# One core, one decoder block: u and y_a with its gate by token, q, k and y_b's gate in merged 512-column matmuls

## The chip, the core and the metric

The kernel runs on one core of one Trainium2 chip. Its time is the device time of one execution in microseconds (us). An execution under the profiler gives a trace: every instruction of the engines with its start and duration. The engines are TensorE (PE, matmuls and transposes), VectorE (DVE), ScalarE (ACT), GpSimd (POOL) and SyncE (SP, which here issues the DMAs of the weights). Each works through its own queue in order and waits on semaphores for the others.

## What is computed

One decoder block for 256 tokens with 1024 features, in float32. Cut to what the change touches:

```python
h = rms_norm(x, norm_mix_g[i])
proj = h @ w_in[i]                       # 1024 x 7168
za_u, za_v, q, k, v_att, g_a, g_b = jnp.split(proj, offsets, axis=-1)
y_a = sgu_mixer(gelu(za_u), gelu(za_v), ...)     # u * (tril(W_s) layer_norm(v) + b), per chunk of 128 tokens
y_b = moba_attention(heads(q), heads(k), heads(v_att), rel_bias)   # 16 heads of 64, causal
merged = sigmoid(g_a) * y_a + sigmoid(g_b) * y_b
x = x + merged @ w_out[i]
x = x + square(relu(rms_norm(x) @ w_ff1[i])) @ w_ff2[i]
gate = sigmoid(rms_norm(x) @ w_ple_gate[i])
x = x + gate * (p[i] @ w_ple_proj[i])
return rms_norm(x, norm_final_g)
```

## The kernel before

**Exact products from three.** Every large matmul is made of operands split into a rounded part and a rest (hi and lo for weights, index 0 and 1 for activations): hi x hi + hi x lo + lo x hi. Weights arrive in tiles of 128 x 2048 (1 MB), 69 of them in the order of the list `ORDER`, on SP's queue (`load_to`, L73). ACT rounds a tile in two pieces of 1024 columns (hi, L84), DVE subtracts (lo, L85). `weights(key, width, ahead=3)` (L95) asks for the tile of a step and has the tiles up to two steps ahead split; there are four buffers for raw tiles and three each for hi and lo.

**Two forms of a projection.** `proj_T` (L215) makes output by feature: the weights stand still, 256 token columns move, three matmuls for each of eight k blocks (`mm3`, L116 to L119), twice 128 features per tile. `proj_tok` (L227) makes output by token: 128 tokens stand still and 512 weight columns move (`tok3`, L121 to L128). The first MLP product (`ff1_mm`, L574) has a third form: by feature, with both parts of the activations moving as one matmul of 512 columns against hi, then 256 columns against lo; ACT copies the 512 sums to SBUF (`z`, L584) and DVE adds the two halves (L606).

**The stages around the change.** (1) v by token (`v_rows`). (2) 1/rms of x is spread over columns by a matmul with ones (L272) and copied to `R0`; u by feature in four `proj_T` calls from x times its gain, each multiplied by R0 on DVE and sent through gelu on ACT. At the same time ACT and DVE make a normalised, split copy of x (`hT`). (3) q in four calls from hT; between them v's layer norm and the spatial mixing (`mix`, L362), which multiplies into u. (4) Two halves J of eight heads each: k in two calls (`keys`), v by token in one `proj_tok` call, then four gate calls (20 is y_a's gate, 24 is y_b's gate). Attention goes in pairs of heads c, four pairs for each half, between the matmuls of the projections (the `mid` functions run on PE between the two feature blocks of a call): scores into the pool `scores` (two buffers of two PSUM banks each), softmax on DVE and ACT (`s`), `att_normalise` on DVE, `att_transpose` on PE with a copy by ACT to `pt`, `att_values` on PE. `merge(j)` adds both gated parts and splits them into `mT`. (5) The output projection, whose accumulators take the banks of the pool `scores` after that is closed (L510), then the MLP and the rest.

PSUM has eight banks: three for projections (`mm`), one `yb`, four for the scores. All queues follow the order in which the code is written.

Of the kernel before, what the change touches and what calls it, by code (L numbers as in the profile page):

```python
# [50 lines left out]
def block_kernel(ctx: ExitStack, tc: tile.TileContext, xt, xk, pt, rows, wst, bsp, rel, buckets, wts, out):  # L51
# [63 lines left out]

    def mm3(o, wh, wl, x, first, last, **kw):  # L116
        nc.tensor.matmul(o, wh, x[:, 0], start=first, stop=False, **kw)  # L117
        nc.tensor.matmul(o, wh, x[:, 1], start=False, stop=False, **kw)  # L118
        nc.tensor.matmul(o, wl, x[:, 0], start=False, stop=last, **kw)  # L119
# [107 lines left out]
    def proj_tok(name, c, x, mid=None):  # L227

        os_ = [bank(shape=(P, 512)) for t in range(2)]
        for i in range(2):  # L230
# [1 line left out]
            for k in range(4):
                tok3(os_, x[:, 4 * i + k], wh[:, k], wl[:, k], i + k == 0, i == 1 and k == 3)
            if i == 0 and mid:
                mid()
        return os_
# [33 lines left out]
    rb = bank("yb", 1)  # L270
    for t in range(2):
        nc.tensor.matmul(rb[:, 0, t * P:(t + 1) * P], ones, dg[:, t], start=True, stop=True)  # L272
    R0 = small.tile([P, S], F32, tag="R", name="R0", bufs=1)
    nc.scalar.activation(R0, rb[:, 0], AF.Copy)


    sgu_a = act.tile([P, 2, D], F32, tag="kT", name="sgu_a")
# [599 lines left out]
```

## Time and profile before

| | |
|---|---|
| median of 3 runs | 429.25 us (429.21 to 429.41) |
| the profiled execution | 429.07 us |
| its span (first to last instruction) | 427.4 us |
| granted TensorE clock, mean | 0.996 |
| TensorE busy | 417.5 us (98%), 2556 matmuls in the records |
| VectorE busy | 278.4 us (65%) |
| ScalarE busy | 233.5 us (55%) |
| DMA | 82.02 MB, mean 192 GB/s |

A busy share of PE says little by itself, because matmuls overlap: the next one starts before the one ahead has ended. The distance between starts is what one costs in a stream. The stages lie in the span as follows: v from 5.9 us, u from 29, q from 53, the two halves of attention from 83 to 188, the output projection to 212, the MLP to 390.

### The profile page before, as it was taken

How to read it: one execution, taken by the hardware profiler on the slowest of the kernel's cores; microseconds unless marked ns; L12 is line 12 of the kernel's file. 1: busy time of each engine (PE TensorE's matmuls, PEld its weight loads, DVE VectorE, ACT ScalarE, POOL GpSimd, SP SyncE). 2: the span in 40 equal slices, each digit the busy share in tenths (PEclk: the TensorE clock that was granted, in tenths of full speed). 3: DMA queues.
4: the chain of work that ended last, by engine and by line, in shares of the span. 5: the costliest groups of instructions: out<-in, count | busy, mean ns of one | idle time of the engine just before them, and what ended most of it. 6: DMA issues, size and time to landing. Idle time of an engine off the chain costs nothing.

```text
span 427.4 us, 6272 instructions
## 1 busy us (share of the span) xinstructions
PE 417.5 (98%) x2556; PEld 370.4 (87%) x2556; DVE 278.4 (65%) x373; ACT 233.5 (55%) x365; POOL 9.4 (2%) x18
## 2 busy tenths in 40 slices
PE   8999999999999999999999999999999999999992
PEld 7789999998999989998888888888888888888882
DVE  3676889675585755945578866666666666646555
ACT  5685544276464555564346666555555555435824
POOL 1001020000000000000000000000000000000001
PEclk9999999999999999999999999999999999999998
DMA  7999539545433444465353676555545455552002
GB/s 268 425 393 393 200 128 383 214 166 198 149 138 120 186 140 163 165 275 185 111 166 115 217 285 224 199 199 196 194 179 186 181 186 184 184 196 87 1 2 98
DMA packets 13692, 82.02 MB, mean 192 GB/s; under 512 B 1541, under 2 KB 1813, under 8 KB 5088
## 3 DMA queue, kind: packets, MB, share of 16 engines
q1 hardware_dynamic: 12384, 78.12, 49.9%
q0 software_dynamic: 848, 2.96, 1.9%
q10 hardware_dynamic: 432, 0.54, 0.4%
q8 instruction: 20, 0.33, 0.3%
q14 instruction: 8, 0.07, 0.0%
HBM read 80.54 MB, written 1.07 MB: 191 GB/s over the span
## 4 chain that ended last, share of the span: by engine, by line
PE 90%; DMA 4%; ACT 2%; issue 1%; DVE 1%; POOL 0%; SPq 0%; POOLq 0%; ACTq 0%
PE mm_t L578 13%; PE mm_t L117 9%; PE mm_t L118 9%; PE mm_t L119 9%; PE mm_t L580 7%; PE y L125 7%; PE y L128 7%; PE y L127 7%; DMA raw<-wts 4%; PE o L125 2%; PE o L127 2%; PE mm_t L125 2%; PE o L128 2%; PE mm_t L128 2%; PE mm_t L127 2%
## 5 line engine op out<-in xcount | busy, mean ns | idle before, releaser
L85 DVE TENSOR_TENSOR lo<-raw,hi 128x1024 fp32r<-128x1024 f32 (+1 forms) x140 | 163.0, 1206 | 66.4 <-ACT hi L84 66.2
L84 ACT ACTIVATE hi<-raw 128x1024 fp32r<-128x1024 f32 (+1 forms) x140 | 138.2, 1038 | 30.8 <-issue 9.5
L117 PE MATMUL mm_t<-hT,hi 128*128 128x256 f32 x256 | 73.9, 289 | 0.1
L118 PE MATMUL mm_t<-hT,hi 128*128 128x256 f32 x256 | 72.4, 283 | 0.0
L119 PE MATMUL mm_t<-hT,lo 128*128 128x256 f32 x256 | 72.3, 283 | 0.0
L578 PE MATMUL mm_t<-xs,hi 128*128 128x512 f32 x248 | 62.4, 392 | 0.0
L578 PEld LDWEIGHTS mm_t<-xs,hi 128*128 128x128 f32 x248 | 45.1, 188 | 8.4
L117 PEld LDWEIGHTS mm_t<-hT,hi 128*128 128x128 f32 x256 | 49.0, 191 | 2.0 <-ACT hi L84 0.6
L118 PEld LDWEIGHTS mm_t<-hT,hi 128*128 128x128 f32 x256 | 49.0, 192 | 0.1
L119 PEld LDWEIGHTS mm_t<-hT,lo 128*128 128x128 f32 x256 | 49.0, 191 | 0.0
L580 PEld LDWEIGHTS mm_t<-xs,lo 128*128 128x128 f32 x248 | 34.2, 190 | 2.7
L584 ACT ACTIVATE z<-mm_t 128x512 f32<-128x512 f32 x31 | 18.1, 593 | 32.1 <-PE mm_t L580 32.1
L580 PE MATMUL mm_t<-xs,lo 128*128 128x256 f32 x248 | 35.0, 282 | 0.0
L606 DVE TENSOR_TENSOR z<-z 128x512 f32<-128x512 f32 x16 | 11.0, 690 | 29.3 <-ACT z L584 29.3
L128 PE MATMUL y<-hi,fs 128*128 128x512 f32 x64 | 24.9, 390 | 0.0
L127 PE MATMUL y<-lo,fs 128*128 128x512 f32 x64 | 24.9, 390 | 0.0
L125 PE MATMUL y<-hi,fs 128*128 128x512 f32 x64 | 19.8, 391 | 0.0
L414 ACT ACTIVATE s<-s,nm 128x256 f32<-128x256 f32 (+1 forms) x32 | 14.2, 444 | 8.6 <-DVE nm L410 8.6
L117 PE MATMUL mm_t<-xg,hi 128*128 128x256 f32 x64 | 18.2, 284 | 0.0
L118 PE MATMUL mm_t<-xg,hi 128*128 128x256 f32 x64 | 18.1, 283 | 0.0
L119 PE MATMUL mm_t<-xg,lo 128*128 128x256 f32 x64 | 18.1, 283 | 0.0
L128 PEld LDWEIGHTS y<-hi,fs 128*128 128x128 f32 x64 | 12.0, 188 | 2.6
(200 smaller groups left out, 670.3 us busy)
## 6 DMA issues: line engine op xcount, KB each, us to landing
raw<-wts SPq DMA_DIRECT2D x67, 1024.0 KB, 4.8
TB<-rvd POOLq DMA_DIRECT2D x1, 2048.0 KB, 15.9
raw<-wts SPq DMA_DIRECT2D x4, 256.0 KB, 5.0
raw<-wts SPq DMA_DIRECT2D x2, 512.0 KB, 6.6
xtok<-xk SPq DMA_DIRECT2D x2, 512.0 KB, 10.0
late<-xk SPq DMA_DIRECT2D x2, 512.0 KB, 6.4
out<-ots SPq DMA_DIRECT2D x3, 256.0 KB, 2.1
xg<-xt SPq DMA_DIRECT2D x1, 512.0 KB, 7.3
```

The costliest lines, as they stand in the source:

```text
L84: nc.scalar.activation(hi[i][:, s], raw[i][:, s], AF.Copy)
L85: nc.vector.tensor_tensor(lo[i][:, s], raw[i][:, s], hi[i].bitcast(F32)[:, s], op=OP.subtract)
L117: nc.tensor.matmul(o, wh, x[:, 0], start=first, stop=False, **kw)
L118: nc.tensor.matmul(o, wh, x[:, 1], start=False, stop=False, **kw)
L119: nc.tensor.matmul(o, wl, x[:, 0], start=False, stop=last, **kw)
L125: nc.tensor.matmul(os_[t], x[:, 0, ts[t]], wh, start=first, stop=False)
L127: nc.tensor.matmul(os_[t], x[:, 0, ts[t]], wl, start=False, stop=False)
L128: nc.tensor.matmul(os_[t], x[:, 1, ts[t]], wh, start=False, stop=last)
L414: nc.scalar.activation(s[:, h, cs], s[:, h, cs], AF.Exp, bias=nm[:, i, h:h + 1], accum_out=sm[:, i, h:h + 1])
L578: nc.tensor.matmul(o, wh[:, k, fs], xs1[:, k], start=k == 0, stop=False, skip_group_check=True)
L580: nc.tensor.matmul(o[:, 0], wl[:, k, fs], xs1[:, k, 0], start=False, stop=k == KD - 1, skip_group_check=True)
L584: nc.scalar.activation(z[:, f], o, AF.Copy)
```

## The change

- **u** is made by token in two `proj_tok` calls (its weight tiles are laid out anew as `w_u`), with gelu and 1/rms (`r0`, one number per token) in ACT's copy. The matmul for R0 moves from the start of u to the middle of its first call (`factor_by_column`).
- **The spatial mixing** works by token as well: the triangular weights stand still, v moves; DVE adds the bias per token (`bcol`) and multiplies by u.
- **q, k and y_b's gate** take the form of the first MLP product (`wide_mm`); they start from x times its gain, and R0 is multiplied in on DVE afterwards. The copy `hT` is gone.
- **y_a's gate** is made by token, one `proj_tok` call for each half (`gate_a`): tanh on ACT, then the product with u on DVE, once for each 128 tokens.
- **Softmax transposes** go into the score banks instead of projection banks; one ACT copy per pair, which also turns the token order around.
- **The merge** transposes u times its gate with PE (four 128x128 blocks for each j) and adds it on DVE to y_b's gated part. It comes later: after the second gate of y_b, after the next half's first k call, and in the output projection.

In the second half the end of ACT's queue, from the tanh of y_a's gate to the last copy of probabilities; before (ta, tb are gates, pt the transposed probabilities, hi split weights):

```order
L449 ACTIVATE tb_1854<-mm_t 128x512
L84 ACTIVATE hi_1870<-raw_1650 128x1024 x2
L107 ACTIVATE mT<-ta_1752 128x2x256
L449 ACTIVATE ta_1939<-mm_t 128x512
L84 ACTIVATE hi_1943<-raw_1684 128x1024 x2
L434 ACTIVATE pt_1974<-mm_t 128x384 x2
L449 ACTIVATE tb_2009<-mm_t 128x512
L434 ACTIVATE pt_2011<-mm_t 128x384 x2
```

The same place of ACT's queue in the changed kernel (z is a gate's sums in SBUF, sp the score banks):

```order
L465 ACTIVATE ta_1534<-mm_t,rh 128x512
L85 ACTIVATE hi_1551<-raw_1374 128x1024 x2
L229 ACTIVATE z_w_gb_1557<-mm_t 128x512 x2
L475 ACTIVATE tb_1596<-z_w_gb_1557 128x512
L85 ACTIVATE hi_1601<-raw_1418 128x1024 x2
L229 ACTIVATE z_w_gb_1607<-mm_t 128x512
L429 ACTIVATE pt_1626<-sp_1490 128x6x128
L229 ACTIVATE z_w_gb_1607<-mm_t 128x512
L475 ACTIVATE tb_1654<-z_w_gb_1607 128x512
L108 ACTIVATE mT<-tb_1596 128x2x256
L429 ACTIVATE pt_1664<-sp_1495 128x6x128
```

The tanh of y_b's gate now reads z and not PSUM, three copies of z are new, and the split of mT stands ahead of the last copy of probabilities.

The same stretch of DVE's queue, from the normalisation of the last two pairs on; before:

```order
L421 RECIPROCAL rc_1862<-sm_1825 128x4
L424 TENSOR_SCALAR s_1819<-s_1819,rc_1862 128x256 x2
L424 TENSOR_SCALAR s_1819<-s_1819,rc_1862 128x128 x2
L85 TENSOR_TENSOR lo_1871<-raw_1650,hi_1870 128x1024 x2
L454 SCALAR_TENSOR_TENSOR ta_1752<-ta_1752,uT 128x512
L455 SCALAR_TENSOR_TENSOR tb_1854<-tb_1854,yb_t 128x512
L457 TENSOR_TENSOR ta_1752<-ta_1752,tb_1854 128x512
L108 TENSOR_TENSOR mT<-ta_1752,mT 128x2x256
L85 TENSOR_TENSOR lo_1944<-raw_1684,hi_1943 128x1024 x2
```

And in the changed kernel (ahead of it, between the softmax and the normalisation, stands the product of u with its gate):

```order
L467 SCALAR_TENSOR_TENSOR u<-ta_1534,u 128x512
L415 RECIPROCAL rc_1537<-sm_1506 128x4
L418 TENSOR_SCALAR s_1500<-s_1500,rc_1537 128x256 x2
L418 TENSOR_SCALAR s_1500<-s_1500,rc_1537 128x128 x2
L415 RECIPROCAL rc_1543<-sm_1517 128x4
L418 TENSOR_SCALAR s_1511<-s_1511,rc_1543 128x256 x2
L418 TENSOR_SCALAR s_1511<-s_1511,rc_1543 128x128 x2
L86 TENSOR_TENSOR lo_1552<-raw_1374,hi_1551 128x1024 x2
L232 TENSOR_TENSOR z_w_gb_1557<-z_w_gb_1557 128x2x256
L473 TENSOR_TENSOR z_w_gb_1557<-z_w_gb_1557,R_315 128x2x256
L478 SCALAR_TENSOR_TENSOR tb_1596<-tb_1596,yb_t 128x512
L86 TENSOR_TENSOR lo_1602<-raw_1418,hi_1601 128x1024 x2
```

The gate's addition and multiplication stand between the splits of two weight tiles.

PE's queue at the end of the second half, with the semaphores of each wait; before:

```order
L433 MATMUL mm_t<-ident,s_1819 128x128 [waits DVE_49,Activation_49]
L433 MATMUL mm_t<-ident,s_1819 128x128 x2
L125 MATMUL o_2030<-hi_1870,mT 128x512
L125 MATMUL o_2031<-hi_1870,mT 128x512
L127 MATMUL o_2030<-lo_1871,mT 128x512 [waits DVE_49]
```

And in the changed kernel:

```order
L485 MATMUL mm_t<-ident,u 128x128 [waits Activation_49]
L485 MATMUL mm_t<-ident,u 128x128 x3
L428 MATMUL sp_1495<-ident,s_1511 128x128 [waits DVE_49]
L428 MATMUL sp_1495<-ident,s_1511 128x128 x2
L121 MATMUL o_1680<-hi_1551,mT 128x512 [waits Activation_49]
L121 MATMUL o_1681<-hi_1551,mT 128x512
L123 MATMUL o_1680<-lo_1552,mT 128x512 [waits DVE_49]
```

Four transposes of u are new there, and the first output matmul (`o`) now waits for ACT.

The core of the diff:

```diff
-ORDER = [("w_v", i) for i in range(4)] + [("w_in", j) for j in (0, 1, 2, 3, 8, 9, 10, 11)]
+ORDER = [("w_v", i) for i in range(4)] + [("w_u", i) for i in range(4)] + [("w_qk", j) for j in range(4)]
...
+    def wide_mm(o, wh, wl, x, f, ks):
+        fs = slice(f * P, (f + 1) * P)
+        for k in ks:
+            nc.tensor.matmul(o, wh[:, k, fs], x[:, k], start=k == 0, stop=False, skip_group_check=True)
+        for k in ks:
+            nc.tensor.matmul(o[:, 0], wl[:, k, fs], x[:, k, 0], start=False, stop=k == KD - 1, skip_group_check=True)
...
+    def proj_T(key, x, mid=None):
+        wh, wl = weights(key, CW)
+        z = wide_out(f"z_{key[0]}{key[1]}")
         for f in range(2):
-            fs = slice(f * P, (f + 1) * P)
-            for k in range(KD):
-                mm3(o[:, f], wh[:, k, fs], wl[:, k, fs], x[:, k], k == 0, k == KD - 1)
+            o = bank()
+            wide_mm(o, wh, wl, x, f, range(KD))
+            nc.scalar.activation(z[:, f], o, AF.Copy)
             if f == 0 and mid:
                 mid()
-        return o
+        nc.vector.tensor_add(z[:, :, 0], z[:, :, 0], z[:, :, 1])
+        return z[:, :, 0]
...
+    proj_tok("w_u", 0, by_token(u, 0, AF.Gelu_apprx_tanh), {0: (v_post,), 2: (factor_by_column, v_stats)})
+    proj_tok("w_u", 1, by_token(u, 1, AF.Gelu_apprx_tanh), {1: (lambda: v_norm(0),), 3: (lambda: v_norm(1),)})
...
     def att_transpose(c):
         s, _ = sc_sb.pop(c)
-        pt_sb[c] = tmp.tile([P, 2, RVW], F32, tag="pt", name=f"pt{c}", bufs=2)
+        pp = sp_.pop(c)
+        pt_sb[c] = tmp.tile([P, 2, 3, P], F32, tag="pt", name=f"pt{c}", bufs=2)
         for h in range(2):
-            pp = bank(shape=(P, 512))
             for d, src in ((0, 256), (1, 0), (2, 128)):
-                nc.tensor.transpose(pp[:, d * P:(d + 1) * P], s[:, h, src:src + P], ident)
-            nc.scalar.activation(pt_sb[c][:, h], pp[:, :RVW], AF.Copy)
+                nc.tensor.transpose(pp[:, h, d * P:(d + 1) * P], s[:, h, src:src + P], ident)
+        nc.scalar.activation(pt_sb[c][:, :, :, ::-1], pp[:, :, :RVW].rearrange("p h (d s) -> p h d s", d=3), AF.Copy)
...
     def keys(j, mid=None):
-        o = proj_h(12, j, mid)
...
-        nc.scalar.activation(kT_[0][:, 2 * j:2 * j + 2], o, AF.Copy)
+        o = proj_T(("w_qk", 4 + j), xg2, mid)
+        nc.vector.tensor_tensor(kT[:, 2 * j:2 * j + 2], o, two_rows(R0), op=OP.mult)
...
+    def gate_a(J, mids):
+        def post(t, o):
+            th = tmp.tile([P, 512], F32, tag="th", name=f"ta{J}{t}", bufs=3)
+            nc.scalar.activation(th, o, AF.Tanh, scale=rh[:, t:t + 1])
+            ut = u[:, t, halves(J)]
+            nc.vector.scalar_tensor_tensor(ut, th, 1.0, ut, op0=OP.add, op1=OP.mult)
+        proj_tok("w_ga", J, post, mids)
+
+    def gate_b(j, mid=None):
+        z = proj_T(("w_gb", j), xg2, mid)
+        nc.vector.tensor_tensor(z, z, two_rows(R0), op=OP.mult)
+        tb[j] = tmp.tile([P, 2, S], F32, tag="th", name=f"tb{j}", bufs=3)
+        nc.scalar.activation(tb[j], z, AF.Tanh, scale=0.5)
...
+    def merge(j):
+        o = bank()
+        for k in range(2):
+            for t in range(2):
+                nc.tensor.transpose(o[:, k, t * P:(t + 1) * P], u[:, t, (2 * j + k) * P:(2 * j + k + 1) * P], ident)
+        nc.vector.scalar_tensor_tensor(tb[j], o, 0.5, tb[j], op0=OP.mult, op1=OP.add)
+        split_act(mT[:, 2 * j:2 * j + 2], tb[j])
...
     for J in range(2):
         a, b, c = 2 * J, 2 * J + 1, 4 * J
-        keys(a, mid=(lambda: value_two(a - 1)) if J else (lambda: mix(3)))
+        keys(a, mid=(lambda: values_b(a - 1)) if J else None)
+        if J:
+            merge(a - 1)
         keys(b, mid=lambda: score_two(c))
         att_normalise(c)
         att_normalise(c + 1)
-        for t, o in enumerate(proj_tok("w_va", J, hT)):
-            nc.scalar.activation(va[:, t, halves(J)], o, AF.Copy)
-        ta[a] = gate_tanh(proj_h(20, a, lambda: att_transpose(c)), f"ta{a}")
-        tb[a] = gate_tanh(proj_h(24, a, lambda: transpose_score(c + 1)), f"tb{a}")
+        proj_tok("w_va", J, by_token(va, J, AF.Copy), {2: (lambda: att_transpose(c),)})
+        gate_a(J, {0: (lambda: att_transpose(c + 1),), 1: (lambda: value_two(a),), 2: (lambda: score_two(c + 2),)})
         att_normalise(c + 2)
         att_normalise(c + 3)
-        ta[b] = gate_tanh(proj_h(20, b, lambda: value_two(a)), f"ta{b}")
-        tb[b] = gate_tanh(proj_h(24, b, lambda: att_transpose(c + 2)), f"tb{b}")
+        gate_b(a)
+        merge_b(a)
+        gate_b(b, mid=lambda: att_transpose(c + 2))
+        merge(a)
         att_transpose(c + 3)
```

## Rows read from the trace of the kernel before

**Rows 1.** The page, busy time (share of the span) and instructions of each engine.

```profile
PE 417.5 (98%) x2556; PEld 370.4 (87%) x2556; DVE 278.4 (65%) x373; ACT 233.5 (55%) x365; POOL 9.4 (2%) x18
```

**Rows 2.** Waits of PE: engine, line, waited for; us in total, times, longest.

```profile
PE yb_t L179 <- DVE mhalf L139: 1.1, 1, 1.1
PE vo L125 <- ACT hi L84: 0.5, 1, 0.5
```

**Rows 3.** Timeline of PE in u: start, duration, instruction; 39 starts apart.

```profile
30.18 0.28 PE L117 MATMUL mm_t<-xg,hi 128*128 128x256 f32 x1
...
34.86 0.28 PE L117 MATMUL mm_t<-xg,hi 128*128 128x256 f32 x1
```

**Rows 4.** Timeline of PE in v, 54 starts apart.

```profile
14.77 0.62 PE L125 MATMUL vo<-hi,xg 128*128 128x512 f32 x2
...
27.01 0.62 PE L125 MATMUL vo<-hi,xg 128*128 128x512 f32 x2
```

**Rows 5.** Chain that ended last, in the first MLP product: start, us, what.

```profile
236.11 1.84 PE mm_t L578 x8
237.95 0.95 PE mm_t L580 x8
```

**Rows 6.** Timeline of PE between v and u, with idle time and releaser.

```profile
28.14 0.39 PE L128 MATMUL vo<-hi,xg 128*128 128x512 f32 x1
28.95 0.68 PE L272 MATMUL yb_t<-dg,ones 128*128 128x128 f32 x4 [0.41 <-DVE dg L266]
```

**Rows 7.** Chain (first two) and timeline of PE: transposes, a bank, scores.

```profile
209.26 0.87 PE mm_t L541 x8
107.17 0.66 PE mm_t L433 x6
132.48 0.82 PE L433 MATMUL mm_t<-ident,s 128*128 128x128 f32 x6
133.38 0.39 PE L117 MATMUL mm_t<-hT,hi 128*128 128x256 f32 x1
114.15 0.70 PE L396 MATMUL sp<-kT,qT 64*128 64x256 f32 x4
...
115.66 0.39 PE L117 MATMUL mm_t<-hT,hi 128*128 128x256 f32 x1
```

**Rows 8.** Timeline of ACT: tanh, split, copies of pt and of z.

```profile
120.39 0.58 ACT L449 ACTIVATE tb<-mm_t 128x512 f32<-128x512 f32 x1
120.86 2.00 ACT L84 ACTIVATE hi<-raw 128x1024 fp32r<-128x1024 f32 x2
133.23 0.87 ACT L434 ACTIVATE pt<-mm_t 128x384 f32<-128x384 f32 x2
237.38 1.06 ACT L584 ACTIVATE z<-mm_t 128x512 f32<-128x512 f32 x2
```

**Rows 9.** Timeline of DVE: softmax, normalisation, split, addition.

```profile
115.12 0.69 DVE L404 SCALAR_TENSOR_TENSOR s<-sp,TB 128x512 f32<-128x512 f32 x1 [0.46 <-PE sp L399]
118.83 0.16 DVE L421 RECIPROCAL rc<-sm 128x4 f32<-128x4 f32 x1
119.03 1.00 DVE L424 TENSOR_SCALAR s<-s,rc 128x256 f32<-128x256 f32 x4
121.94 2.36 DVE L85 TENSOR_TENSOR lo<-raw,hi 128x1024 fp32r<-128x1024 f32 x2 [0.21 <-ACT hi L84]
238.83 0.69 DVE L606 TENSOR_TENSOR z<-z 128x512 f32<-128x512 f32 x1
```

**Rows 10.** Timeline of PE at the start; windows: PE, PEld, DVE, ACT, POOL busy, PEclk, DMA.

```profile
1.12 4.26 PE L179 MATMUL yb_t<-ones 128*128 128x128 f32 x22 [1.12 <-DVE mhalf L139]
...
418.00:420.00 2.00, 1.59 (x14) 1.39 (x12) 1.93 (x4) 1.47 (x4) 0.00 (x0) 1.00 0.00 0
423.00:425.00 2.00, 0.00 (x0) 0.00 (x0) 0.36 (x1) 0.33 (x1) 0.00 (x0) 0.81 0.85 323
425.00:427.40 2.40, 0.00 (x0) 0.00 (x0) 0.00 (x0) 0.00 (x0) 0.00 (x0) 0.50 0.25 94
```

More of the change, by code (lines that the diff above doesn't have):

```diff
@@ L114, in low_part @@
         nc.vector.scalar_tensor_tensor(dst[:, 1], src, g, dst[:, 0].bitcast(F32), op0=OP.mult, op1=OP.subtract)
[L116 to L119, printed above, removed]
     def tok3(os_, x, wh, wl, first, last):
@@ L231, in proj_tok @@
             wh, wl = weights((name, 2 * c + i), 512)
[L232 to L236, printed above, removed]
+            for t in range(2):
+                ts = slice(t * P, (t + 1) * P)
+                for k in range(4):
+                    kk = 4 * i + k
+                    nc.tensor.matmul(os_[t], xg2[:, kk, 0, ts], wh[:, k], start=kk == 0, stop=False)
+                    nc.tensor.matmul(os_[t], xg2[:, kk, 0, ts], wl[:, k], start=False, stop=False)
+                    nc.tensor.matmul(os_[t], xg2[:, kk, 1, ts], wh[:, k], start=False, stop=kk == KD - 1)
+                if i:
+                    post(t, os_[t])
+                for f in mids.get(2 * i + t, ()):
+                    f()
     v = act.tile([P, 2, D], F32, tag="t8a", name="v")
@@ L268, in block_kernel @@
     split_to(6)
[L270 to L277, printed above, removed]
+    sgu = act.tile([P, KD, S], F32, tag="kT", name="sgu")
+    wsT = sgu[:, :4].rearrange("p k s -> p (k s)").rearrange("p (g t) -> p g t", g=8)
     ln_g, ln_b = [act.tile([P, D], F32, tag="ln", name=n, bufs=2) for n in ("ln_g", "ln_b")]
-    wsT = sgu_a[:, 0].rearrange("p (g t) -> p g t", g=8)
@@ L303, in normalise_x @@
-    def normalise_x(a):
-        xr = tmp.tile([P, 2, S], F32, tag="sq", name=f"xr{a}")
-        for k in range(2):
-            kk = 2 * a + k
-            nc.vector.scalar_tensor_tensor(xr[:, k], xT[:, kk], gcol[:, 0, kk:kk + 1], R0, op0=OP.mult, op1=OP.mult)
-        split_act(hT[:, 2 * a:2 * a + 2], xr)
-    def v_post(c):
-        for t in range(2):
-            nc.scalar.activation(v[:, t, halves(c)], vo[c][:, t], AF.Gelu_apprx_tanh, scale=r0[:, t:t + 1])
+    R0 = small.tile([P, S], F32, tag="R", name="R0", bufs=1)
@@ new lines, in block_kernel, with factor_by_column, v_post @@
+    rh = small.tile([P, 2], F32, tag="rh", name="rh", bufs=1)
+    nc.vector.tensor_scalar(rh, r0, 0.5, None, op0=OP.mult)
+    def factor_by_column():
+        rb = bank("yb", 1)
+        for t in range(2):
+            nc.tensor.matmul(rb[:, 0, t * P:(t + 1) * P], ones, dg[:, t], start=True, stop=True)
+        nc.scalar.activation(R0, rb[:, 0], AF.Copy)
+    def v_post():
+        for c in range(2):
+            for t in range(2):
+                nc.scalar.activation(v[:, t, halves(c)], vo[c][:, t], AF.Gelu_apprx_tanh, scale=r0[:, t:t + 1])
@@ L528, in block_kernel @@
             if i + k == 0:
-                value_two(3)
+                values_b(3)
+            elif i == 1 and k == 0:
+                merge(3)
     x2 = act.tile([P, 2, D], F32, tag="t8a", name="x2")
```

161 lines of the change are left out of this document (60 added, 101 removed).

## The prediction

> **What bounds the kernel now.** I read the page's busy times first: TensorE (PE) is busy for 98% of the span, VectorE (DVE) for 65%, ScalarE (ACT) for 55% [rows 1]. A modelled busy time can hide waits, so the list of PE's waits came next: it has three entries, 1.1, 0.5 and 0.4 us, all before 29 us [rows 2, 6]. So PE is never held up by another engine in the middle of the run, and the span is PE's instruction stream, one matmul after the other, with some 6 us ahead of it and 8 us behind. Two things can therefore move the time: what the stream holds, priced by the distance from one matmul's start to the next (the duration column counts overlapped time), and a wait that is put into the stream. ACT and DVE matter only where PE comes to wait for them.
>
> **The matmuls.** Matmuls with 256 moving columns: 39 starts in 4.68 us, 0.120 us each [rows 3]. With 512 columns: 54 starts in 12.24 us, 0.2267 us each [rows 4]. Two short ones cost 0.240, one long one 0.227. In u and y_a's gate 8 calls of 48 short matmuls become 4 calls of 48 long ones: 384 x 0.120 - 192 x 0.2267 = 46.1 - 43.5 = -2.6 us. In q, k and y_b's gate each of 24 half tiles goes from 24 short matmuls (2.88) to 8 long and 8 short, the form that the first MLP product has already: 1.84 + 0.95 = 2.79 us [rows 5]. 24 x 0.09 = -2.1 us. Together -4.7. Both new forms stand in this trace, so I leave this term little room: 4.4 to 5.2.
>
> The Trainium skill (TensorE: Matmul & The Clock Gate, section on the back-to-back issue gap) puts a warm gap at N/2.4 ns plus 2.5 ns, so that merging would save 2.5 ns per matmul taken out; the rows show 13 ns (2 x 120 - 227). By the page 384 matmuls fewer are worth 1.0 us, not 4.7, and the transposes below would eat it.
>
> **What else enters or leaves the stream.** The matmul that spreads 1/rms over columns stood between v and u and waited for DVE: 28.14 to 28.95 is 0.81 us where 0.23 is due [rows 6]. It now stands inside u's product, 8 us later: -0.58. Four groups of four 128x128 transposes are new, eight take 0.87 [rows 7]: 4 x 0.435 = +1.74. Six softmax transposes take 0.66; one group in each half waits for a matmul bank, 132.48 to 133.38 = 0.90 [rows 7], and as transposes now go into the score banks that falls away: I count one, -0.24. The mixing matmuls, scores and values keep their number. Sum so far: -4.7 - 0.6 + 1.7 - 0.2 = **-3.8 us**.
>
> **What costs nothing, and what covers it.** The normalised copy of x disappears from ACT and DVE in the u stage; PE waited for neither there, so nothing is won. Each feature-first projection gains an ACT copy of 0.5, a DVE addition of 0.7 and a DVE multiplication, which I price as the addition [rows 8, 9]. In the q and k stages a half tile lasts 2.8, a tile 5.6, weights are split two tiles ahead, and the split takes DVE 2.4 and ACT 2.0 [rows 8, 9]; the additions fit. The tightest place is k: copy, addition, product and handovers end 2.4 us after a tile, and the scores come half a tile (2.79) after it, 0.4 spare. If a split runs late there, the scores wait about 1 us in each half.
>
> **The wait that is added.** In each half the fourth pair's probabilities are transposed right after the second gate of y_b, and ACT's copy of them (pt) now stands last in a serial ACT-DVE chain. I follow the chain and PE from the start of the score matmuls of pairs three and four, t = 0, in us.
>
> PE [rows 4, 5, 7]: scores 1.5 (114.15 to 115.66); the last quarter of y_a's gate 12 x 0.227 = 2.7; both gates of y_b 4 x 2.79 = 11.2; two groups of softmax transposes 1.3; the merge's transposes 0.4. PE is through at 17.1 to 17.2.
>
> ACT and DVE [rows 8, 9]: before the softmax DVE must do u's gate product, which waits for the tanh on ACT: 0.25 + 0.6 + 0.7, softmax at 1.5 (before, it began 0.97 after the scores began, 114.15 to 115.12). From there to the end of the exponentials 5.27 (115.12 to 120.39): 6.8. Then, in the order of the queues: tanh of the second token half 0.6 (ACT), product 0.7, two normalisations of 0.2 + 1.0 each, split of lo 2.3, addition 0.7, multiplication 0.7 (DVE): 14.3. Tanh 0.5, split of hi 2.0, copies 0.5 (z), 0.8 (pt of pair three), 0.6 (z) on ACT: 18.7. Addition and multiplication 1.4, tanh 0.6, copy of mT 0.6, and pt of pair four 0.8: **22.2**. Two copies of 384 take 0.87; for one of 768 I take 0.8, between a half of that and ACT's 1.0 for 1024 columns.
>
> Before, DVE had no gate product between softmax and normalisation, no addition and multiplication in the gates, and pt came right behind one tanh, so nothing waited. After the first half PE goes on with k's first half tile (2.8) and the values of pair three (0.75, half of the like score group): 17.2 + 0.1 for the bank of z + 3.6 = 20.9, then waits for pt until 22.2: **+1.4**. After the second half the next matmuls are the output projection's. Their accumulators take over the score banks, whose last reader is now pt's copy: PE is idle from 17.2 to 22.2: **+5.0**. Bounds: the chain has 20.7 us of work behind t = 1.5; with the softmax at 0.97, and each pt copy at 0.5 it is 1.1 shorter, with 1.0 for each pt and 0.3 more in handovers 0.7 longer. So 3.9 to 5.7 at the end and 0.3 to 2.1 in the middle. I take 5.0 and 1.4, which come from the nearest row at every step.
>
> Behind the waiting matmul stands the whole rest of the kernel; the queues of SP and POOL are untouched (the weight stream keeps its order of one tile per step, the broadcast of the bias becomes a small load).
>
> **Sum.** -3.8 + 1.4 + 5.0 = +2.6. The profiled execution took 429.07 (span 427.4): 431.7. It lies 0.18 under the median of 429.25, so the forecast is **431.9**. A measurement here can tell about 0.2%, 0.86 us, from no change.
>
> **Rivals.**
> *The clock falls in the idle stretch (slower still).* PE's last matmul starts before 420, and the granted clock is 1.00 there; in 423 to 425 its mean is 0.81, from 425 on 0.50 [rows 10]: it fell at about 424.2, some 4.7 us after the last matmul. The new idle stretch is 5.0 us, hardly longer. If it falls, matmuls run at 1.2 GHz until it rises again. For the price I have one stretch that looks like it: the first 22 matmuls, 128 columns each, take 4.26 us, 0.194 each [rows 10], against 0.11 for the 128 columns of a transpose: 22 x 0.084 = 1.85 us too long, though the granted clock reads 1.00 there. +1.9 gives 433.8; I allow up to 435. For: the length. Against: one sighting only, at the end of the run.
> The Trainium skill (TensorE: Matmul & The Clock Gate, Part 1) says that an idle PE goes back to 1.2 GHz and must be busy to be released; the rows agree as to the fall.
>
> *The chain is covered (faster).* The price of the added waits hangs on one length: if pt of pair four is there 17.2 us after the scores and not 22.2, both waits are gone and the stream's -3.8 is left: 425.4. It decides at a chain 5 us shorter, which needs two of its steps (a split and the normalisations, say) out of the way. Against: both queues are in order, and each step has its row. In between, a chain 2 to 3 us shorter leaves 1.5 to 4 us of waits: 427 to 429.5.
>
> *More waits (slower).* The scores behind k come 1 us late in both halves: 433.9. For: 0.4 spare. Against: ACT has nothing else queued there. It lies with the first rival in time.
>
> *Matmuls do not gain what the rows say.* By the page's gap 3.7 us less: 435.6. Against: both forms were timed here.
>
> **How the numbers follow.** Forecast (two waits, clock stays): 0.46, 430.4 to 433.2. Clock falls: 0.20, up to 435. More waits: 0.07. Page's gap: 0.02. Shorter chain: 0.14, 427 to 430. Covered: 0.11, 425 to 427. For 8 in 10 the range leaves out the covered case and the top: 427.6 to 434.9. Faster than 428.4: 0.11 and half of the shorter chain, less the small part of it that ends higher, 0.16. Within 428.4 to 430.1: the rest of the shorter chain and the low edge of the forecast, 0.15. Slower: 0.69.
>
> **What would show it.** Right: starts 0.227 apart in u, 2.79 us per half tile in q, k and the gate; an idle stretch of PE of about 5 us just ahead of the first output matmul, put down to ACT's copy of pt, one of 1 to 1.5 in k's third tile; ACT and DVE nearly without gaps in y_b's gates. Wrong: PE without idle stretches (chain), a granted clock under 1 behind the long one (clock), waits of score matmuls for kT, or 512-column starts further apart than 0.23.

## The result: 433.6 us, slower by 0.9%

The changed kernel took **433.61 us** (median of 4, 432.29 to 433.82) against 429.25: a ratio of 1.0094, 95% interval 1.0074 to 1.0115. The forecast was 431.9 with a range of 427.6 to 434.9, and the rival in which the clock falls too was put at 433.8. The profiled execution is the shortest of the four: 432.29, span 430.6 (before 427.4), at a mean granted TensorE clock of 0.993. The other three have 0.987 and spans of 431.7 to 432.1, so the rows below show the mildest case.

The page's line of busy times, then the three largest entries of the list of PE's waits (engine, line, waited for; us in total, times, longest), both of the changed kernel:

```profile
PE 416.6 (97%) x2188; PEld 352.5 (82%) x2188; DVE 285.1 (66%) x390; ACT 240.4 (56%) x369; POOL 10.4 (2%) x19
```

```profile
PE o L121 <- ACT pt L429: 4.3, 1, 4.3
PE yb_t L175 <- DVE mhalf L135: 1.1, 1, 1.1
PE yb_t L440 <- ACT pt L429: 0.7, 1, 0.7
```

PE issues 368 matmuls fewer than in [rows 1] and is busy 0.9 us less, yet the span is 3.2 us longer. Two entries (the first and the third) stand nowhere in [rows 2], and both name ACT's copy of pt. The wait of the 1/rms matmul [rows 6] is gone.

Timeline of PE at the end of the second half, with idle time and releaser in brackets; the first row is the start of the score matmuls from which the prediction counted (t = 0):

```profile
168.05 0.70 PE L390 MATMUL sp<-kT,qT 64*128 64x256 f32 x4
...
184.23 0.60 PE L485 MATMUL mm_t<-ident,u 128*128 128x128 f32 x4
184.66 0.82 PE L428 MATMUL sp<-ident,s 128*128 128x128 f32 x6
189.75 1.22 PE L121 MATMUL o<-hi,mT 128*128 128x512 f32 x2 [4.27 <-ACT pt L429]
190.77 0.63 PE L123 MATMUL o<-lo,mT 128*128 128x512 f32 x1
191.20 0.63 PE L124 MATMUL o<-hi,mT 128*128 128x512 f32 x1
...
193.01 0.40 PE L123 MATMUL o<-lo,mT 128*128 128x512 f32 x1
193.25 0.39 PE L124 MATMUL o<-hi,mT 128*128 128x512 f32 x1
```

The six softmax transposes take 0.57 us of the stream (from start to start in the first half, 129.24 to 129.81), so PE is through at 185.23, 17.2 after t = 0, and starts again at 189.75: 4.5 us of idleness. Behind it stands what the forecast's sum left out: the output matmuls start 0.43 apart up to 192.5, and 0.23 apart from 193 on. The windows of the same stretch (busy time of PE, PEld, DVE, ACT, POOL, then the mean granted clock, DMA share and GB/s) say why:

```profile
185.00:189.00 4.00, 0.48 (x5) 0.24 (x3) 3.05 (x4) 2.46 (x6) 0.00 (x0) 1.00 1.02 383
189.00:190.00 1.00, 0.25 (x1) 0.25 (x2) 0.69 (x1) 1.00 (x3) 0.00 (x0) 0.60 0.99 418
190.00:192.00 2.00, 2.00 (x5) 1.58 (x6) 1.32 (x2) 1.59 (x2) 0.00 (x0) 0.50 0.14 57
192.00:193.00 1.00, 1.00 (x4) 0.77 (x3) 1.00 (x1) 0.00 (x0) 0.00 (x0) 0.69 0.00 0
```

A mean of 0.60 in 189 to 190 puts the fall at 189.2, the 0.69 in 192 to 193 the rise at 192.6. From 189.75 to 192.6 PE works at the lower of its two levels (1.2 instead of 2.4 GHz), where starts lie nearly twice as far apart: half of 2.9, some 1.4 us, is lost. By the Trainium skill (TensorE: Matmul & The Clock Gate, section "Wait — 56ns, not 53.3ns?") back-to-back matmuls of 512 columns at the low level start 426.7 ns apart. The trace agrees: 190.77 to 191.20 is 0.43 us.

The middle, k's third tile, in the timeline of PE:

```profile
132.79 0.66 PE L440 MATMUL yb_t<-pt,va 128*64 128x256 f32 x4
...
134.33 0.66 PE L440 MATMUL yb_t<-pt,va 128*64 128x256 f32 x4 [0.67 <-ACT pt L429]
...
135.14 1.20 PE L215 MATMUL mm_t<-xg,hi 128*128 128x512 f32 x4
```

From the first value matmul to the next product 2.35 us pass; the kernels below without this wait take 1.50. So 0.85 is lost.

The end of the chain, ACT's timeline:

```profile
187.83 0.63 ACT L475 ACTIVATE tb<-z_w_gb 128x512 f32<-128x512 f32 x1 [1.54 <-DVE z_w_gb L473]
188.37 0.63 ACT L108 ACTIVATE mT<-tb 128x512 fp32r<-128x512 f32 x1
188.91 0.79 ACT L429 ACTIVATE pt<-sp 128x768 f32<-128x768 f32 x1
```

The copy of pt, last of all, ends at 189.70, and PE's first output matmul follows at once.

Where the stream got shorter, PE's timeline in u (36 starts from the first to the second row) and in q (a half tile from the third row to the fifth):

```profile
28.36 0.39 PE L245 MATMUL mm_t<-hi,xg 128*128 128x512 f32 x1
...
36.29 0.39 PE L247 MATMUL mm_t<-hi,xg 128*128 128x512 f32 x1
...
54.32 2.00 PE L215 MATMUL mm_t<-xg,hi 128*128 128x512 f32 x8
56.16 1.11 PE L217 MATMUL mm_t<-xg,lo 128*128 128x256 f32 x8
57.11 1.06 PE L366 MATMUL mm_t<-v,sgu 128*128 128x128 f32 x8
```

7.93 us for 35 distances is 0.227; the half tile lasts 2.79. Both are the prices taken from [rows 4, 5].

### The profile page after: what moved, and what is told of

It is laid out like the page before. It is cut to its first block, busy times and chain, and to the rows that moved or that the text cites. A ratio compares the mean times of both kernels' runs of the same rounds, so it can differ in the third digit from the quotient of the medians.

```text
span 430.6 us, 5546 instructions
## 1 busy us (share of the span) xinstructions
PE 416.6 (97%) x2188; PEld 352.5 (82%) x2188; DVE 285.1 (66%) x390; ACT 240.4 (56%) x369; POOL 10.4 (2%) x19
## 4 chain that ended last, share of the span: by engine, by line
PE 86%; ACT 6%; DVE 5%; issue 2%; DMA 1%; POOLq 0%; POOL 0%; ACTq 0%
PE mm_t L215 20%; PE mm_t L217 10%; PE y L121 7%; PE y L124 7%; PE y L123 7%; PE mm_t L245 5%; PE mm_t L247 5%; PE mm_t L246 5%; PE o L121 2%; PE vo L123 2%; PE o L123 2%; PE o L124 2%; PE vo L121 2%; ACT s L408 2%; PE vo L124 2%
## 5 line engine op out<-in xcount | busy, mean ns | idle before, releaser
L215 PE MATMUL mm_t<-xg,hi 128*128 128x512 f32 x192 | 49.2, 398 | 0.0
L215 PEld LDWEIGHTS mm_t<-xg,hi 128*128 128x128 f32 x192 | 34.6, 189 | 7.3 <-issue 0.8
L245 PE MATMUL mm_t<-hi,xg 128*128 128x512 f32 x96 | 38.3, 399 | 0.0
L247 PE MATMUL mm_t<-hi,xg 128*128 128x512 f32 x96 | 37.5, 391 | 0.0
L246 PE MATMUL mm_t<-lo,xg 128*128 128x512 f32 x96 | 37.5, 390 | 0.0
L583 ACT ACTIVATE z<-mm_t 128x512 f32<-128x512 f32 x31 | 18.1, 594 | 32.1 <-PE mm_t L217 32.1
L217 PEld LDWEIGHTS mm_t<-xg,lo 128*128 128x128 f32 x192 | 26.2, 190 | 2.0
L217 PE MATMUL mm_t<-xg,lo 128*128 128x256 f32 x192 | 26.8, 282 | 0.0
L245 PEld LDWEIGHTS mm_t<-hi,xg 128*128 128x128 f32 x96 | 18.0, 188 | 4.0 <-issue 0.3
L247 PEld LDWEIGHTS mm_t<-hi,xg 128*128 128x128 f32 x96 | 18.0, 188 | 3.8
L246 PEld LDWEIGHTS mm_t<-lo,xg 128*128 128x128 f32 x96 | 18.1, 188 | 3.4
L229 ACT ACTIVATE z_w_qk<-mm_t 128x512 f32<-128x512 f32 x16 | 9.5, 593 | 18.9 <-PE mm_t L217 14.8
```

Of the source, the lines that this page charges most:

```text
L215: nc.tensor.matmul(o, wh[:, k, fs], x[:, k], start=k == 0, stop=False, skip_group_check=True)
L217: nc.tensor.matmul(o[:, 0], wl[:, k, fs], x[:, k, 0], start=False, stop=k == KD - 1, skip_group_check=True)
L245: nc.tensor.matmul(os_[t], xg2[:, kk, 0, ts], wh[:, k], start=kk == 0, stop=False)
L246: nc.tensor.matmul(os_[t], xg2[:, kk, 0, ts], wl[:, k], start=False, stop=False)
L247: nc.tensor.matmul(os_[t], xg2[:, kk, 1, ts], wh[:, k], start=False, stop=kk == KD - 1)
L583: nc.scalar.activation(z[:, f], o, AF.Copy)
```

## The experiments

The theory to be tested: the new form of the matmuls saves some 3.8 us as priced, and three things give more back: the wait for pt in the middle (0.85), the one at the end (4.5), and the lower clock behind the long one. All ratios are to the kernel before, timed on the same chip (medians 429.3 to 429.4).

**1. The copy earlier.**

```
-        gate_b(b, mid=lambda: att_transpose(c + 2))
+        gate_b(b, mid=lambda: (att_transpose(c + 2), att_transpose(c + 3)))
         merge(a)
-        att_transpose(c + 3)
```

> The fourth pair's probabilities are transposed together with the third's, in the middle of y_b's second gate, so that ACT copies them ahead of that gate's tanh and of the merge. Theory of waits and clock: by the rows of the changed kernel the copy ends 3.1 us earlier (186.6 instead of 189.7), so the idle stretch ahead of the first output matmul shrinks from 4.5 to about 1.4 us, the 0.85 us in k's third tile goes, and the granted clock stays 1.00 there (1.4 us of slow matmuls gone in the profiled execution): span about 425.3, time 426.5 to 428. Theory of waits without the clock (slow first matmuls have another cause): about 428.5 to 430. Rival, the first output matmul waits for something other than this copy: no change, 433.6.

Measured 426.91, ratio 0.9943 (0.9931 to 0.9956), span 425.2. PE's timeline at the end:

```profile
184.00 0.60 PE L485 MATMUL mm_t<-ident,u 128*128 128x128 f32 x4
185.68 0.72 PE L121 MATMUL o<-hi,mT 128*128 128x512 f32 x2 [1.08 <-ACT pt L429]
186.25 0.40 PE L123 MATMUL o<-lo,mT 128*128 128x512 f32 x1
```

The merge's transposes take 0.35 here, so 1.3 us of idleness are left, the matmuls behind it start 0.23 apart, and the wait in the middle is gone. The mean clock is 0.994 to 0.997 in all 5 executions, as in the kernel before. One call moved turns the change from slower into faster: the waits and the clock behind them, not the new forms, were the loss.

**2. The idle stretch filled.**

```
+    spare = bank(shape=(P, 512))
+    h0 = hi[POS["w_out", 0]]
+    for i in range(17):
+        nc.tensor.matmul(spare, xg2[:, 0, 0, :P], h0[:, :512], start=True, stop=True)
```

> 17 matmuls of 512 columns (3.9 us) into a spare bank are put ahead of the first output matmul; their result is read by nobody. The chain to the copy of pt is untouched, so the first output matmul should start where it did (4.5 us after the transposes). Theory that idleness lets the clock fall: the granted clock stays 1.00, the output matmuls start 0.227 apart from the first on, 431 to 432.2 in place of 433.6. If the slow first matmuls have another cause: 433.6 and 0.427 apart as before. If PE was not idle but waiting on a queue of its own: the fillers push everything back and it is 437.

Measured 431.02, ratio 1.0044 (1.0030 to 1.0057), span 429.3.

```profile
185.33 4.15 PE L533 MATMUL mm_t<-hi,xg 128*128 128x512 f32 x17
189.86 0.73 PE L122 MATMUL o<-hi,mT 128*128 128x512 f32 x2 [0.38 <-ACT pt L430]
190.43 0.40 PE L124 MATMUL o<-lo,mT 128*128 128x512 f32 x1
```

The first output matmul stands where it stood (4.53 us after the transposes), but PE was at work, the clock stayed at 1.00, and the matmuls start 0.23 apart. Work that nobody reads makes the kernel faster: by 1.3 us between the two profiled executions, by 2.6 between the medians (the ratios differ by 0.50%, 2.1 us). That is the clock's price by itself; it differs between executions.

**3. The copy twice.**

```
+        for _ in range(2 if c % 4 == 3 else 1):
             nc.scalar.activation(pt_sb[c][...], pp[...], AF.Copy)
```

> ACT copies the fourth pair's transposed probabilities twice in each half (0.8 us more at the end of the chain). Theory of the chain: the wait in k's third tile grows from 0.85 to 1.65 and the idle stretch ahead of the output projection from 4.5 to 5.3: 435.2, a little more if a longer idle stretch costs a longer stretch at the lower clock. Rival, the waits are set by the weights' split or by banks: under 0.3 of change, 433.6 to 433.9.

Measured 435.12, ratio 1.0132 (1.0118 to 1.0146): 1.5 more than the change. The list of waits has 1.5 in the middle (0.7 in the change) and 5.1 at the end (4.3): 0.8 in each, as the chain has it. The windows after the idle stretch, which ends at 191.64 here:

```profile
189.00:190.00 1.00, 0.00 (x0) 0.00 (x0) 0.38 (x1) 1.00 (x3) 0.00 (x0) 0.61 0.93 393
190.00:196.00 6.00, 4.36 (x10) 3.48 (x11) 3.05 (x3) 3.44 (x5) 0.00 (x0) 0.50 0.31 100
196.00:197.00 1.00, 1.00 (x7) 0.51 (x7) 0.00 (x0) 0.00 (x0) 0.00 (x0) 0.97 0.55 90
```

The lower clock lasts from 189.2 to 196.0 here, twice as long as in the profiled execution of the change.

**4. Other banks first.**

```
-        tag=f"acc{2 * t + c}"      # c0: the first 512 columns
+        tag=f"acc{2 * c + t}"
...
+    for w, i in ((w0, 0), (w1, 1)):
+        for k in range(2):
+            out_mm(i, k, 0, w)     # 24 matmuls of the first 512 columns, then the values
```

> The output accumulators of the first 512 columns take over the third pair's score bank, those of the second 512 columns the fourth pair's, and the first 24 output matmuls (5.4 us) are all of the first 512 columns; the copy of the fourth pair's probabilities stays last in the chain. Theory that the wait is only the taking over of the bank: the first output matmul waits until the third pair's copy (185.8 in the rows, 0.6 us of idleness in place of 4.5), pt is there before the values need it, the clock stays: span about 425.3, time 426.5 to 428. Rival, all accumulators wait for the last reader of the whole pool, or for the values: 433 to 434.

Measured 432.64, ratio 1.0078 (1.0065 to 1.0092), span 430.8. A miss for the theory as I had put it:

```profile
189.76 1.05 PE L121 MATMUL o<-hi,mT 128*128 128x512 f32 x2 [4.28 <-ACT pt L429]
```

If the tiles of the new pool lie in the order of their names (no trace shows where they lie), the first accumulators here are in the banks of the third pair, whose copy is done 4 us earlier. The wait is where it was, so it does not look like a wait for one bank; run 5 settles it. The clock fell here too, at 190.0, just after PE was back at work, and rose at 193.4.

**5. The same order, the score pool left open.**

```
-    scores.__exit__(None, None, None)
-    acc = acc_tiles("o")
+    pair = [ps_scores.tile([P, 2, 512], F32, tag="scores", name=f"o{c}") for c in range(2)]
+    acc = [[pair[c][:, t] for t in range(2)] for c in range(2)]
```

> Same order of output matmuls as in the run with the bank order (first 24 of the first 512 columns), but the output accumulators are tiles of the score pool itself, so that each takes over one score tile instead of the closed pool's space as a whole. Theory that the first output matmul waited for the release of the whole pool: it now waits only for the third pair's copy (about 185.8 in the rows, 0.6 us after PE is through), the values find the fourth pair's copy done (189.7 against 191.2), the clock stays 1.00: 426.5 to 428. Rival, it is a bank or port that PE and ACT share, or the weights: 432 to 434.

Measured 426.90, ratio 0.9948 (0.9936 to 0.9961).

```profile
185.12 0.82 PE L428 MATMUL sp<-ident,s 128*128 128x128 f32 x6
186.31 0.73 PE L121 MATMUL o<-hi,mT 128*128 128x512 f32 x2 [0.36 <-ACT pt L429]
```

0.6 us of idleness instead of 4.5. Runs 4 and 5 have the same order of matmuls and differ in the pool that the accumulators come from. Here tiles of a new pool on a closed pool's space waited for the last reader of the closed pool as a whole (4.5 us of idleness), tiles of the same pool only for the tile whose place they take (0.6).

**6 and 7. Both copies ahead of the tanh.** In run 6 both groups of transposes stand right behind the matmuls of y_b's first gate; in run 7 the fourth pair's stand eight long matmuls later, inside the second gate. In both, ACT copies pt before the first gate's tanh. The calls as run 6 has them (run 7's edit is longer):

```
-        gate_b(a)
+        gate_b(a, behind=lambda: (att_transpose(c + 2), att_transpose(c + 3)))
         merge_b(a)
-        gate_b(b, mid=lambda: att_transpose(c + 2))
+        gate_b(b)
         merge(a)
-        att_transpose(c + 3)
```

> Both groups of softmax transposes of pairs three and four stand right behind the matmuls of y_b's first gate, so ACT copies them before that gate's tanh, while it would wait for VectorE. Theory of the chain: the normalisation of pair four ends some 0.4 us after PE gets there, so PE waits about 0.4 to 0.5 in each half and nowhere else: the stream's gain of 3.8 less 0.9, so 426.2 (425.6 to 426.8). Rival, ScalarE's two copies push the tanh and the later merge so that the waits come back at the merge's transposes or at the output matmuls: 427.5 to 429.

> Pair three's transposes stand behind the matmuls of y_b's first gate, pair four's between the long and the short matmuls of the first half of the second gate, 1.8 us later, and both copies still ahead of the first gate's tanh on ACT. Theory of the chain: no wait of PE is left in either half, the stream's gain of 3.8 us stays whole: 425.4 (425.0 to 426.0). Rival as for the kernel before it: the copies delay the tanh, and the waits come back further on: 427 to 429.

Measured 425.73 (ratio 0.9917, 0.9904 to 0.9931) and **425.56** (0.9914, 0.9900 to 0.9927), spans 424.0 and 423.8. Of PE's waits only the one at the very start (1.1, for mhalf) is left in either. Run 6 does not even wait the 0.4 I had put down for the normalisation: with the third pair's transposes ahead of them, the fourth pair's come late enough. ACT's timeline of the change (one row), then of run 7:

```profile
182.09 0.63 ACT L475 ACTIVATE tb<-z_w_gb 128x512 f32<-128x512 f32 x1 [3.32 <-DVE z_w_gb L473]
```

```profile
178.05 0.81 ACT L429 ACTIVATE pt<-sp 128x768 f32<-128x768 f32 x1
180.56 0.82 ACT L429 ACTIVATE pt<-sp 128x768 f32<-128x768 f32 x1 [1.70 <-PE sp L428]
```

The copies fill the time in which ACT stands waiting for DVE's product in the changed kernel (3.3 us ahead of the first gate's tanh), and cost nothing. These are the fastest kernels of this study, faster than the kernel before and the changed one.

**8. The merged matmuls alone.** The kernel before, with k and both gates in 24 merged half tiles, each with its copy z on ACT and an addition on DVE:

```
-        return proj_T(("w_in", c0 + j), hT, mid=mid)
+            for k in range(KD):
+                nc.tensor.matmul(o, wh[:, k, fs], hT[:, k], ...)
+            for k in range(KD):
+                nc.tensor.matmul(o[:, 0], wl[:, k, fs], hT[:, k, 0], ...)
+            nc.scalar.activation(z[:, f], o, AF.Copy)
```

> The kernel before with one part of the change alone: k and both gates by feature with merged 512-column matmuls, an ACT copy and a VectorE addition for each, 24 half tiles; u, q and the by-feature order stay. Price by the rows: 24 x (2.88 - 2.79) = 2.1 us less, 427.1, if everything else is covered. Theory of the chain: the copy of the fourth pair's probabilities now stands behind an addition and the tanh that waits for it, and 0.5 to 2 us of new waits appear ahead of the values: 427.5 to 429. Rival, the merging itself brings nothing in place: 429.3 or more without waits.

Measured 441.27, ratio 1.0282 (1.0265 to 1.0299): no theory had that. PE's timeline in the second half, and ACT's of the same stretch:

```profile
189.09 0.49 PE L433 MATMUL mm_t<-ident,s 128*128 128x128 f32 x3
190.72 0.55 PE L433 MATMUL mm_t<-ident,s 128*128 128x128 f32 x3 [1.14 <-ACT z L473]
194.60 3.32 PE L469 MATMUL mm_t<-hT,hi 128*128 128x512 f32 x8 [3.33 <-ACT z L473]
```

```profile
189.55 0.63 ACT L107 ACTIVATE mT<-ta 128x512 fp32r<-128x512 f32 x1 [3.44 <-DVE ta L457]
190.09 0.58 ACT L473 ACTIVATE z<-mm_t 128x512 f32<-128x512 f32 x1
...
192.07 1.99 ACT L84 ACTIVATE hi<-raw 128x1024 fp32r<-128x1024 f32 x2
```

A merged half tile fills a whole matmul bank and keeps it until ACT's z copy. The softmax transposes take two more of the three banks, and the z copies stand in ACT's queue behind a merge that waits 3.44 for DVE, then behind a split of 2.0. By the starts PE is idle for 4.9 us in each half (the list of waits for z has 9.0 in all, counted from the modelled ends of matmuls), and the clock falls behind each: the 8 matmuls at 194.60 last 3.3, where 8 of that length last 2.0 in q's rows above.

**9. Merged matmuls, transposes in the score banks.**

```
+        sp = sp_.pop(c)
         for h in range(2):
-            pp = bank(shape=(P, 512))
+            pp = sp[:, h]
```

> The run with the merged k and gates alone, and in addition the softmax transposes in the score banks in place of matmul banks, as the whole change has them. Theory that its 12 us were the three matmul banks: the two waits of 4 to 5 us of transposes and matmuls for ACT's z copies go from both halves, and so does the lower clock behind them; what is left is the chain, whose last link is again the copy of pt ahead of the output accumulators, 3.5 to 4.5 us after PE, with 1.4 to 2.5 us of lower clock: 431 to 435 in place of 441.3. Rival, ScalarE is simply too slow with the additional copies: 439 to 441.

Measured 451.46, ratio 1.0515 (1.0488 to 1.0542), worse still and by a fault of the experiment. The list of PE's waits:

```profile
PE sp L434 <- ACT pt L435: 18.1, 8, 4.5
```

Both heads lie in one tile now, so the second head's transposes wait until ACT has copied the first head's. The run says nothing on the banks.

**11. The same with one copy of both heads**, after all six transposes:

```
         for h in range(2):
             for d, src in ((0, 256), (1, 0), (2, 128)):
-                nc.tensor.transpose(pp[:, d * P:(d + 1) * P], ...)
-            nc.scalar.activation(pt_sb[c][:, h], pp[:, :RVW], AF.Copy)
+                nc.tensor.transpose(pp[:, h, d * P:(d + 1) * P], ...)
+        nc.scalar.activation(pt_sb[c], pp[:, :, :RVW], AF.Copy)
```

> As the last run with merged k and gates alone and score banks, but the six transposes of a pair come first and one ACT copy of both heads follows, so that no transpose waits for a copy of the same tile. Theory that the 22 us of that run were the 8 waits of the second head's transposes for the first head's copy (18.1 in its list of waits), and the 12 us of merging alone the three matmul banks: both go, what is left is the chain and the lower clock behind it, 430 to 435. Rival, ScalarE cannot keep up with the additional copies: over 438.

Measured 435.56, ratio 1.0142 (1.0127 to 1.0156): just above the 430 to 435 of the bank theory, which thus missed its range by 0.6, and well below the rival's 438. The z waits and the 18.1 are gone; the list now begins (score matmuls also wait 1.2 once for kT, further down):

```profile
PE o L125 <- ACT pt L434: 3.4, 1, 3.4
PE sp L396 <- ACT pt L434: 1.7, 2, 0.9
```

The first is the change's own end wait. The second, which I had not foreseen, is the price of the score banks in this order of work: the next scores want the tile from which pt is still being copied. The change as a whole avoids that by its other order.

**10. The split behind the copy.**

```
-        gate_b(b, mid=lambda: att_transpose(c + 2))
+        gate_b(b, mid=lambda: att_transpose(c + 2), ahead=2)
         merge(a)
         att_transpose(c + 3)
+        split_to(POS["w_gb", b] + 3)
```

> The changed kernel, but the weight split that stands in ACT's and VectorE's queues at y_b's second gate (2.0 and 2.36 us) comes after the copy of the fourth pair's probabilities; nothing else is moved. Theory of the chain: the copy ends some 1.8 us earlier (187.9 against 189.7 in the rows; then the matmuls of the gate, which end at 183.8, set it), the idle stretch ahead of the output matmuls shrinks from 4.5 to 2.7, the 0.85 us in k's third tile goes, the clock stays 1.00: 433.6 - 1.8 - 0.85 - 1.4 to 2.5 = 428.5 to 429.5. If the clock falls all the same: 430 to 431. Rival, the split that is late is missed by k or by the output projection: 432 or more.

Measured 430.89, ratio 1.0030 (1.0015 to 1.0045), in 12 runs from 428.90 to 432.23. The wait in the middle is gone, the one at the end is 3.3. PE's timeline and two windows of the profiled execution:

```profile
184.24 0.82 PE L428 MATMUL sp<-ident,s 128*128 128x128 f32 x6
188.07 1.00 PE L121 MATMUL o<-hi,mT 128*128 128x512 f32 x2 [3.01 <-ACT pt L429]
```

```profile
188.00:189.00 1.00, 0.93 (x3) 0.77 (x4) 0.05 (x2) 1.00 (x3) 0.00 (x0) 0.68 0.00 0
...
191.00:192.00 1.00, 1.00 (x4) 0.84 (x3) 1.00 (x2) 0.80 (x1) 0.00 (x0) 0.61 0.00 0
```

The copy ends 1.7 earlier (188.0 against 189.7), as the chain has it; I had not reckoned with PE being through 0.4 earlier too (184.8). The clock fell at 188.4, 0.3 after PE had gone back to work. Of the 12 executions four have spans of 427.2 to 428.0 at a mean clock of 0.994, as much as the kernel before; eight have 428.8 to 430.5 at 0.987 to 0.993. Without the fall the sum would give 427.1 (427.4 - 3.6 + 3.3). So with 3.3 us of idleness the clock seems to fall in some executions and not in others, and that would spread the times; only one execution, with the fall, was traced.

**12. The merging undone in the fastest kernel.** Run 7, with 24 short matmuls per half tile in q, k and y_b's gate, all else as it was:

```
-                nc.tensor.matmul(o, wh[:, k, fs], xg2[:, k], ...)              # 512 columns
+                nc.tensor.matmul(o[:, 0], wh[:, k, fs], x[:, k, 0], ...)       # 256 columns
+                nc.tensor.matmul(o[:, 1], wh[:, k, fs], x[:, k, 1], ...)
```

> The fastest kernel so far (both transposes ahead, no waits) with one thing undone: in q, k and y_b's gate each 512-column matmul is two of 256 again, 24 short matmuls per half tile instead of 8 long and 8 short; copies, additions and banks stay. By the rows' price, 24 half tiles of 0.09 us: 2.1 us slower, 427.7 in place of 425.56. Rival, by a gap of 2.5 ns per matmul: 24 x 8 x 2.5 ns = 0.5, 426.0. Rival, order of the weights loaded matters more than the length: outside 425.8 to 428.2.

Measured 427.50, ratio 0.9957 (0.9943 to 0.9970): 1.94 slower than run 7. A tile of q with its mixing matmuls lasts, in run 7 and then in run 12:

```profile
57.14 1.06 PE L366 MATMUL mm_t<-v,sgu 128*128 128x128 f32 x8
...
63.62 1.06 PE L366 MATMUL mm_t<-v,sgu 128*128 128x128 f32 x8
```

```profile
57.57 1.06 PE L378 MATMUL mm_t<-v,sgu 128*128 128x128 f32 x8
...
64.22 1.06 PE L378 MATMUL mm_t<-v,sgu 128*128 128x128 f32 x8
```

6.48 against 6.65: 0.17 for two half tiles, 24 x 0.085 = 2.0. An estimate by the Trainium skill's warm gap of N/2.4 + 2.5 ns (TensorE: Matmul & The Clock Gate, section "Back-to-back issue gap") would have made it 192 x 2.5 ns = 0.5. The measurement decides for the rows.

**The account.** Spans of the profiled executions against the 427.4 of before. The stream's term is run 7, where PE waits for nothing new: 423.8 - 427.4 = -3.6. The waits are read from the timelines, the clock's term is half of the time that PE worked at the lower level.

| Kernel | stream | wait, middle | idle, end | clock | sum | measured |
|---|---|---|---|---|---|---|
| the change | -3.6 | 0.85 | 4.5 | 1.4 | +3.2 | +3.2 |
| 1, copy earlier | -3.6 | 0 | 1.3 | 0 | -2.3 | -2.2 |
| 2, filled | -3.6 | 0.85 | 4.5 | 0 | +1.8 | +1.9 |
| 3, copy twice | -3.6 | 1.7 | 5.4 | 2.2 | +5.7 | +5.8 |
| 4, other banks | -3.6 | 0.85 | 4.5 | 1.7 | +3.5 | +3.4 |
| 5, pool open | -3.6 | 0.85 | 0.6 | 0 | -2.2 | -1.6 |
| 10, late split | -3.6 | 0 | 3.3 | 1.7 | +1.4 | +1.7 |

The other four executions of run 5 have spans of 425.1 to 425.5, -2.3 to -1.9, around the sum.

## Why the prediction was right, and what it missed

**The direction and its mechanism were right.** PE's stream, priced by starts, and a serial chain of ACT and DVE that ends in the copy of pt: run 1 takes the waits away by one moved line, run 3 adds 0.8 to each by one more copy, runs 6 and 7 leave the stream's gain alone. The sum was +2.6; the profiled execution has +3.2.

**The stream: -3.8 forecast, -3.6 measured** (run 7 by its profiled execution; the medians 429.38 and 425.56 give -3.8). Its parts stand in the rows: 0.227 apart in u, 2.79 per half tile, 0.43 for a group of merge transposes, no stall between v and u (28.13 to 28.36 is one distance), no bank wait ahead of k's third tile. The merged part alone is worth 1.94 (run 12) where 2.1 was put down. The by-token part (-2.6) was not measured in a run of its own. In u it can be read from the traces: from the last matmul of v to the one behind u PE took 24.45 us before (28.14 to 52.59) and takes 22.54 now (28.13 to 50.67), 1.9 less, where 0.6 for the 1/rms matmul and 1.3 for the long form were priced.

**PE through at 17.2: to the tenth** (168.05 to 185.23).

**The chain: 22.2 forecast, 21.65 measured** (168.05 to 189.70), hence 4.5 at the end instead of 5.0 and 0.85 in the middle instead of 1.4; both lie in the bounds. No single step was off. The softmax starts at 1.44 (forecast 1.5), DVE's multiplication of the first gate is done at 13.9 (14.3), the last z copy ahead of the additions at 18.2 (18.7), pt at 21.65 (22.2). I had added durations, and the start of the next instruction on the same engine comes a little before the end of the one before it: on ACT's rows above, tanh, mT and pt last 0.63, 0.63 and 0.79, but start 0.54 apart. It is the same trap that the prediction avoided on PE.

**Who waits at the end: right by luck.** The prediction said that the accumulators take over the score banks, whose last reader is the copy of pt. Run 4 gave the first accumulators other tiles and the wait stayed; run 5 kept the pool and it went. What is waited for is the last reader of the closed pool, and that happened to be the same copy.

**The clock: the step that failed.** The forecast case was "two waits, clock stays", with 0.46 against 0.20 for the fall. The row behind it [rows 10] had shown the clock at half some 4.7 us after the last matmul, and the forecast idle stretch was 5.0. I called that "hardly longer" and took the single sighting for a limit that might not be reached, though by my own numbers it was. Run 2 shows that idleness is the cause, run 10 that 3.3 us can already bring the fall (traced in one execution, and by spans and mean clocks in 8 of 12), run 1 that 1.3 did not by the mean clocks of its 5. The price, 1.9, came out of the right size: 1.4 in the profiled execution, 2.1 to 2.6 by run 2 at the median. That is luck, since it was taken from the first 22 matmuls, whose granted clock reads 1.00, and from none at the lower level. From the forecast to the median the sum is 0.2 (stream) - 0.55 - 0.5 (chain) + 2.1 to 2.6 (clock) = 1.3 to 1.8, and 433.6 - 431.9 = 1.7 was measured. With the fall as the likeliest case the forecast would have been 433.8.

**The other rivals.** The chain covered (425.4, chance 0.11) did not happen here but is what runs 6 and 7 build, at 425.7 and 425.6. "More waits", the scores behind k, did not come: the list of waits has no such entry. "Matmuls do not gain what the rows say" is refuted for the merged matmuls by run 12: 1.94 us, where the rows give 2.1.

**What stays open.** The lower clock lasted 3.4 us in the traced executions of the change and of runs 4 and 10, and 6.8 in that of run 3; why was not settled. The three slower executions of the change have mean clocks (0.987) that fit the longer one, but were not traced. In run 8 little is left over: -2.1 for the merging, 9.9 of idleness by the starts and 3.4 for two stretches of the lower clock (half of 6.8 us) make +11.2, and its span has +11.4.

## What to carry to other kernels

Where one engine is busy for 98%, making its stream shorter by 4 us is worth 4 us (run 7) only if no wait stands at its seams: follow the serial chain of the other engines to each place where the busy engine needs its last link, by starts and not by durations, and put copies that free a buffer into the time in which their engine waits anyway (run 7: the same work, 8 us less than the change). Price an idle stretch of PE as itself plus the lower clock behind it, which here came with 3.3 us and more and not with 1.3. A part of a change need not work alone: the merged matmuls that save 2 us in the changed kernel cost 12 in the kernel before. Other banks for the transposes give 5.7 of that back (run 11); the rest are the waits that are left in run 11's list and the lower clock behind them.
